# Hybrid encoder block: contraction groups of 2, 4, 4, 4, 2 row blocks, silu(c) from a replicated row, x turned in parts

## The chip, the core and the metric

The kernel runs on one core of a Trainium2 chip. The metric is the time of one execution on the device, in microseconds (us); less is better. Engines are named as in the profile: PE multiplies matrices, DVE and ACT work on vectors, SP issues the DMAs.

## What is computed

One encoder layer on 256 tokens of 2048 channels, in float32:

```python
mod = silu(c) @ w_ada + b_ada                       # 6 parts of 2048
sh1, sc1, gt1, sh2, sc2, gt2 = split(mod, 6)
h = rmsnorm(x, g_pre_mix) * (1 + sc1) + sh1
proj = h @ w_in                                     # 10752 columns
# HGRN2 on q, f_fwd, f_bwd, i, g (1024 columns each) -> y_a
# windowed attention on q, k, v                      -> y_b
y = (sigmoid(gate_a) * y_a + sigmoid(gate_b) * y_b) @ w_out
x = x + gt1 * rmsnorm(y, g_post_mix)
h = rmsnorm(x, g_pre_ffn) * (1 + sc2) + sh2
y = expert_choice_ffn(h)                            # 16 experts, 32 tokens each
x = x + gt2 * rmsnorm(y, g_post_ffn)
```

## The kernel before

**Weights** come as 1 MB tiles (128 partitions, 2048 floats each), each into one of 25 slots, through one DMA queue that SP issues. The list `prog` is the order of use and of loading. "A" tiles are blocks of `w_ada` for shift and scale of the first norm, "B" tiles are blocks of the other four parts, "W" tiles hold 4 row blocks (of 128 rows) of 512 columns of `w_in`.

**Modulation.** `ada` (L399) multiplies an A or B tile with silu(c) and sums along the row, on DVE. silu(c) stands on all partitions (`CR`): `expand` (L293) makes it from a column array by four products on PE that ACT copies out (L298). It does so at the start and once more in the last expert, where the last four B tiles are used.

**Start.** `norm_x` squares both halves of x on ACT (L323), scales all of x (L330, ACT), transposes it on PE (L334) and copies it out (L336, ACT), giving `nT`. `rotary` makes the angle tables (DVE lines around L382, two sines on ACT). `mod_gain` (L404, L406) finishes shift and scale, and `make_h` applies them for the row blocks of one group (L416 on ACT) and splits the result into an upper and a lower part (L417 on ACT, L418 on DVE).

**First stage.** The contraction has 16 row blocks, taken in groups by `GRP`. In each group ten chunks of 512 columns (`EARLY`: f0, b0, f1, b1, q0, q1, hg0, hg1, v0, v1) are multiplied. A weight tile is split by `split`, per 1024 floats: ACT casts the upper part (L433), DVE subtracts the lower (L434), into one of four ring slots. `prod` makes three passes on PE (L181) into one of two PSUM pairs that alternate. The sum is then evicted to a slab (L766, ACT); in later groups it is first reloaded from the slab (L763, ACT); in the last group the eviction applies sigmoid or silu (L768), except for v0 and v1. The A tiles of the next group's row blocks are spread over the chunks of a group; before the first group stand the 8 A tiles of its own. The last group carries 8 B tiles instead.

**After it** come HGRN2 (`hgrn`, from L503, with scans on DVE at L507) beside the other chunks of `w_in`, attention, the branches, the router and the 16 experts.

Programs are scheduled: the order of each engine's instructions is fixed before the run, and is in parts not that of the source. Every engine works through its own list in order.

Of the kernel before, what the change touches and what calls it, by code (L numbers as in the profile page):

```python
# [22 lines left out]
D = 2048  # L23
T = 256
NT = 2
# [14 lines left out]
GRP = [4, 4, 4, 4]  # L40
# [6 lines left out]
# column constants: one [128, W] array  # L47
# [8 lines left out]
# w_in chunks of 512 columns: (kind, first column); "t" comes out as channels x tokens  # L56
# [14 lines left out]
CHUNKS = EARLY + LATE  # L71


class Mem:
    """SBUF in slots of 8 KB per partition; every tenant of a slot is its own tile, and a
    tenant's first write is issued after the one of the tenant before it. A tile gets the
    slot that has been free for longest, so that its load can run ahead."""
# [30 lines left out]
class Ring:  # L108
    """slots that serve one kind of tile in turn"""
# [18 lines left out]
def block_kernel(ctx: ExitStack, tc: tile.TileContext, x, cols, pos, ident_in, hmask, bmask, smask, w_ada, w_in, w_a, w_b, w_out, w_r, w_gu, w_dn, out):  # L128
# [9 lines left out]
    # ---------------- PSUM: two pairs of banks, a ring of three banks, one more bank  # L138
# [16 lines left out]
    # ---------------- stream of weight tiles, 1 MB each, in the order of use  # L155
# [27 lines left out]
    # ---------------- constants  # L183
# [6 lines left out]

    ident = cp.tile([128, 128], F32, name="ident")
# [20 lines left out]
    def table(name="natural_log_exp_and_others"):  # L212
        """the table of ScalarE for what follows on it"""
        S.preload_act_table_set(name)

    def rsqrt(ss, n):
        """sums of D squares -> 1 / rms: exponential of the logarithm, one Newton step"""
        l, r, t, v = tiny(n), tiny(n), tiny(n), tiny(n)
        S.activation(l, ss, AF.Ln, scale=1.0 / D, bias=epsc)
        S.activation(r, l, AF.Exp, scale=-0.5)  # L220
        V.tensor_scalar(v, ss, 1.0 / D, EPS, ALU.mult, ALU.add)
        V.tensor_tensor(t, r, r, ALU.mult)
        V.scalar_tensor_tensor(t, t, -0.5, v, ALU.mult, ALU.mult)
# [6 lines left out]
    prog = [("X",)]  # L230
# [6 lines left out]
    for g in range(NG):  # L237
# [6 lines left out]
        nt, ne = len(todo), len(EARLY)  # L244
        for i, n in enumerate(EARLY):
            prog.append(("W", n, G0[g], GRP[g]))
            k = min(nt, (i + 1) * nt // (ne - NA0)) - min(nt, i * nt // (ne - NA0))
            prog += todo[:k]
            todo = todo[k:]
        prog += todo  # L250
    def mix(items, n, m):
        """items with the next n of the ada tiles spread over the first m"""
# [16 lines left out]
    def src(it):  # L269
        k = it[0]  # L270
        if k in "AB":
            return w_ada[it[1], it[2]]
        if k == "W":
            return w_in[CHUNKS.index(it[1]), it[2] // 4]
        return {"YA": w_a, "YB": w_b, "O": w_out}[k][it[1], it[2]]

    stream += [src(it) for it in prog if it[0] not in "HX"]
# [7 lines left out]
    def spread(c4, w, b=None):  # L285
        """four columns -> their 512 values along the free axis, on all partitions, in a bank"""
# [6 lines left out]
    def expand(c16, name):  # L293
        """a [128, 16] column array -> the 2048 values along the free axis, on all partitions"""
# [7 lines left out]
    # ---------------- x -> n = x / rms(x), transposed  # L302
# [7 lines left out]
    # silu(c) on every partition  # L310
    sig = tiny(16)
    S.activation(sig, col("c"), AF.Sigmoid)
    V.tensor_tensor(sig, sig, col("c"), ALU.mult)
    CR = expand(sig, "crow")
# [3 lines left out]
    def norm_x():  # L318
        for tt in range(NT):
            nc.sync.dma_start(X[tt], x[tt])  # L320
        scr = mem.get([D], F32, "sq")
        for tt in range(NT):
            S.activation(scr, X[tt], AF.Square, accum_out=ssq[:, tt:tt + 1])  # L323
        mem.put(scr)
        rs = rsqrt(ssq, NT)
        for k2 in range(8):
            if k2 % 2 == 0:
                for tt in range(NT):
                    xp = X[tt][:, 256 * k2:256 * k2 + 512]
                    S.activation(xp, xp, AF.Copy, scale=rs[:, tt:tt + 1])  # L330
# [5 lines left out]
            S.copy(NTl[k2 // 4][:, 2 * (k2 % 4):2 * (k2 % 4) + 2, :].rearrange("p a b -> p (a b)"), b)  # L336
        mem.put(*X)
# [9 lines left out]
    # lower bounds of the forget gates: softmax over the two depths  # L347
# [19 lines left out]
    # rotary tables: cos, sin per token  # L367
# [25 lines left out]
    # ---------------- modulation columns  # L393
# [3 lines left out]
    def ada(p, k, t):  # L397
        """block k of 128 channels of modulation part p"""
# [40 lines left out]
    def prod(ps, parts, kind, lhh, lhl, k0, first, last):  # L439
        """ps += (row blocks from k0 of the activations)^T (weight tile)"""  # L440
# [24 lines left out]
    # ---------------- slabs: outputs of the input projection  # L465
# [18 lines left out]
    # ---------------- HGRN2: two heads (half hf) of chunk i  # L484
    def hgrn(i, hf):
# [47 lines left out]
        for j in range(2):  # L533
# [6 lines left out]
            # scores of both directions, transposed: within the chunks, and from one chunk of a pair to the other  # L540
# [17 lines left out]
            # keys scaled to the end of the pair, queries to its start  # L558
# [23 lines left out]
        # per-head norm over the channels (partitions), gate  # L582
# [40 lines left out]
    def heads_t(x3, h, o):  # L623
        """channels x tokens of heads h, h+1 of a token-major slab"""
# [69 lines left out]
    # ---------------- the run through the weight tiles before the experts  # L694
# [146 lines left out]
    for it in prog:  # L841
# [7 lines left out]
        if it[0] == "X":  # L849
            norm_x()  # L850
# [11 lines left out]
        else:  # L862
            pend.append((it, split(t)))
# [9 lines left out]
    # ---------------- residual, second norm  # L873
# [31 lines left out]
    # ---------------- router  # L905
# [41 lines left out]
    def gather(e):  # L947
        """the 32 rows of expert e: channels x rows, normed, with gain and shift"""
# [23 lines left out]
    def combine_weights(e):  # L972
        # combine weights [4 copies of 32 slots, tokens]
# [18 lines left out]
    # ---------------- experts  # L992
    for e in range(NE):
        if e == NE - 1:
            JK = RT[:, 192:704].rearrange("p (t c) -> p t c", t=2)
            sf8 = tiny(16).rearrange("p (t c) -> p t c", t=2)
            CR = expand(sig, "crow")
# [34 lines left out]
        for cb in range(8):  # L1032
# [4 lines left out]
            # 256 columns: sums over a quarter of the rows each in the four groups of 32 partitions,  # L1037
            # which the combine adds up
# [27 lines left out]
    # ---------------- second residual  # L1066
# [37 lines left out]
def finish_deps(tc, nc, mem, mark, pairs):  # L1104
    """the order of a slot's tenants; a table's load stays between its neighbours on ScalarE"""
# [28 lines left out]
def layout(inputs):  # L1134
# [23 lines left out]
    def chunks(w, starts):  # L1158
# [4 lines left out]
    win = chunks(f("w_in").reshape(D, -1), [CH[n][1] for n in CHUNKS])  # L1163
# [16 lines left out]
        "x": f("x").reshape(NT, P, D), "cols": cols, "pos": posn, "ident": np.eye(P, dtype=np.float32),  # L1180
        "hmask": hm, "bmask": bmk, "smask": smk, "w_ada": ada, "w_in": win, "w_a": w_a,
# [21 lines left out]
```

## Time and profile before

| what | us |
|---|---|
| median of 3 runs | 1747.77 |
| lowest, highest | 1747.76, 1747.88 |
| the profiled execution, from first to last instruction | 1746.1 |
| outside this span (median less span) | 1.67 |
| PE busy | 1442.9 |
| DVE busy | 782.3 |
| ACT busy | 555.9 |

The profiled execution's own time is 1747.8 when the 1.67 us outside its span are added, so its span stands for the median. The page's slices show three parts: up to some 830 us PE is busy in nearly every slice, and DMA in 60 to 100% of them; from there to the end DMA is busy without a gap at 419 GB/s while PE waits part of the time. In the first slice of 44 us the engines wait for each other.

### The profile page before, as it was taken

How to read it: one execution, taken by the hardware profiler on the slowest of the kernel's cores; microseconds unless marked ns; L12 is line 12 of the kernel's file. 1: busy time of each engine (PE TensorE's matmuls, PEld its weight loads, DVE VectorE, ACT ScalarE, POOL GpSimd, SP SyncE). 2: the span in 40 equal slices, each digit the busy share in tenths (PEclk: the TensorE clock that was granted, in tenths of full speed). 3: DMA queues.
4: the chain of work that ended last, by engine and by line, in shares of the span. 5: the costliest groups of instructions: out<-in, count | busy, mean ns of one | idle time of the engine just before them, and what ended most of it. 6: DMA issues, size and time to landing. Idle time of an engine off the chain costs nothing.

```text
span 1746.1 us, 24226 instructions
## 1 busy us (share of the span) xinstructions
PE 1442.9 (83%) x10230; PEld 924.5 (53%) x10230; DVE 782.3 (45%) x1048; ACT 555.9 (32%) x865; POOL 0.2 (0%) x4
## 2 busy tenths in 40 slices
PE   4999999999999999997877777776867777677674
PEld 2989997789999998862322312221322232122212
DVE  7777788999977897443111101111111111011115
ACT  6467776655564444441200100000000001000012
POOL 0000000000000000000000000000000000000000
PEclk8999999999999999998998879888897879788987
DMA  9978966766978788776999999999999999999996
GB/s 388 419 293 321 345 255 234 271 245 272 351 271 356 309 352 323 303 306 269 419 419 419 420 419 419 420 420 419 419 419 420 419 419 419 419 419 419 419 419 254
DMA packets 88796, 633.98 MB, mean 363 GB/s; under 512 B 9968, under 2 KB 10480, under 8 KB 11888
## 3 DMA queue, kind: packets, MB, share of 16 engines
q1 hardware_dynamic: 88688, 632.44, 89.7%
q8 instruction: 80, 1.31, 0.3%
q14 instruction: 28, 0.23, 0.0%
HBM read 630.30 MB, written 2.10 MB: 362 GB/s over the span
## 4 chain that ended last, share of the span: by engine, by line
PE 44%; DMA 43%; DVE 8%; ACT 3%; issue 2%; SPq 0%; DVEq 0%; ACTq 0%
PE PS L181 43%; DMA w<-in_w_gu_dram 32%; DMA w<-in_w_dn_dram 9%; DVE w L399 2%; DVE hl L434 1%; DMA w<-in_w_ada_dram 1%; ACT ew L1048 1%; ACT hl L433 1%; DVE F L507 0%; DMA w<-in_w_in_dram 0%; PE PS L1020 0%; ACT ew L1017 0%; DVE x L1086 0%; PE PS L681 0%; PE PS L892 0%
## 5 line engine op out<-in xcount | busy, mean ns | idle before, releaser
L181 PE MATMUL PS<-w,rt 128*32 128x512 f32 x2048 | 325.4, 711 | 141.4 <-DMA w<-in_w_gu_dram 140.1
L181 PE MATMUL PS<-hh,hl 128*128 128x256 f32 x2048 | 383.1, 287 | 13.2 <-ACT hl L433 8.9
L181 PE MATMUL PS<-hl,hl 128*128 128x256 f32 (+1 forms) x1184 | 356.7, 301 | 0.0
L434 DVE TENSOR_TENSOR hl<-w,hl 128x1024 fp32r<-128x1024 f32 x232 | 281.1, 1223 | 118.9 <-ACT hl L433 118.7
L181 PEld LDWEIGHTS PS<-hh,hl 128*128 128x128 f32 x2048 | 324.8, 194 | 15.5 <-ACT hl L433 9.3
L433 ACT CAST hl<-w 128x1024 fp32r<-128x1024 f32 x232 | 241.1, 1048 | 164.8 <-PE PS L181 156.5
L181 PEld LDWEIGHTS PS<-w,rt 128*32 128x32 f32 x2048 | 55.7, 116 | 368.2 <-DMA w<-in_w_gu_dram 301.3
L181 PEld LDWEIGHTS PS<-hl,hl 128*128 128x128 f32 x1184 | 228.7, 193 | 7.2 <-issue 0.7
L399 DVE SCALAR_TENSOR_TENSOR w<-w,crow 128x2048 f32<-128x2048 f32 x96 | 218.8, 2285 | 7.6 <-DMA w<-in_w_ada_dram 4.8
L181 PE MATMUL PS<-ew,rt 128*128 128x256 f32 x512 | 157.7, 434 | 70.0 <-ACT ew L1048 70.0
L1059 DVE TENSOR_TENSOR acc<-acc,PS 128x512 f32<-128x512 f32 x120 | 82.5, 688 | 261.4 <-PE PS L181 261.4
L181 PEld LDWEIGHTS PS<-ew,rt 128*128 128x128 f32 x512 | 94.2, 204 | 146.6 <-ACT ew L1048 137.9
L181 PE MATMUL PS<-w,ew 128*32 128x256 f32 x2048 | 151.5, 415 | 13.9 <-DVE ew L1026 13.9
L1048 ACT COPY ew<-PS 128x256 f32<-128x256 f32 x128 | 47.5, 371 | 259.5 <-PE PS L181 259.5
L1026 DVE TENSOR_TENSOR ew<-ew,PS 128x256 f32<-128x256 f32 x16 | 6.7, 421 | 235.2 <-ACT ew L1025 235.2
L181 PE MATMUL PS<-hl,hh 128*128 128x512 f32 x320 | 103.8, 401 | 5.3 <-DVE hl L434 2.9
L952 DVE TENSOR_SCALAR rt<-ct,rt,small 128x32 f32<-128x32 f32 x32 | 9.4, 300 | 208.4 <-PE PS L181 208.3
L181 PEld LDWEIGHTS PS<-w,ew 128*32 128x32 f32 x2048 | 56.7, 115 | 85.8 <-issue 47.5
L958 ACT COPY ew<-PS 128x512 f32<-128x512 f32 x15 | 8.8, 586 | 268.2 <-PE PS L181 268.2
L1017 ACT COPY ew<-PS 128x512 f32<-128x512 f32 x16 | 9.4, 586 | 232.5 <-PE PS L181 232.5
L181 PE MATMUL PS<-hl,mh 128*128 128x512 f32 x256 | 81.1, 396 | 0.8 <-ACT hl L433 0.7
L181 PEld LDWEIGHTS PS<-hl,hh 128*128 128x128 f32 x320 | 60.1, 191 | 19.9 <-DVE hl L434 4.9
(243 smaller groups left out, 1191.0 us busy)
## 6 DMA issues: line engine op xcount, KB each, us to landing
w<-in_w_gu_dram SPq DMA_DIRECT2D x256, 1024.0 KB, 19.9
w<-in_w_dn_dram SPq DMA_DIRECT2D x128, 1024.0 KB, 19.9
w<-in_w_ada_dram SPq DMA_DIRECT2D x96, 1024.0 KB, 7.0
w<-in_w_in_dram SPq DMA_DIRECT2D x84, 1024.0 KB, 7.4
w<-in_w_out_dram SPq DMA_DIRECT2D x16, 1024.0 KB, 10.6
w<-in_w_a_dram SPq DMA_DIRECT2D x8, 1024.0 KB, 6.5
w<-in_w_b_dram SPq DMA_DIRECT2D x8, 1024.0 KB, 8.3
x<-in_x_dram SPq DMA_DIRECT2D x4, 1024.0 KB, 8.1
```

Source lines behind the costliest of these rows:

```text
L181: E.matmul(o, l, r, start=start, stop=stop, skip_group_check=True, **kw)
L399: V.scalar_tensor_tensor(t, t, 1.0, CR, ALU.mult, ALU.mult, accum_out=MOD[:, p, k:k + 1])
L433: S.copy(hl[:, 0, :], w)
L434: V.tensor_tensor(hl[:, 1, :], w, hl[:, 0, :].bitcast(F32), ALU.subtract)
L952: V.tensor_scalar(oh[:, tt, :], io, pm3[:, tt, e:e + 1], r2[:, tt:tt + 1], ALU.is_equal, ALU.mult)
L958: S.copy(g, b)
L1017: S.copy(gu, b)
L1026: V.tensor_tensor(he, sl_, b3[:, :, 64:128], ALU.mult)
L1048: S.copy(y, b[:, :256])
L1059: V.tensor_tensor(a, a, p3, ALU.add)
```

## The change

- `GRP` is 2, 4, 4, 4, 2 in place of 4, 4, 4, 4: five groups, the first and the last of two row blocks.
- In the groups of two a weight tile holds two row blocks of two chunks ("P" items, `w_e2`, built on the host): one load and one `split` feed the products of a pair of chunks. The groups of four use `w_e4`, tiles as before.
- 4 A tiles stand ahead of the first group. The 8 of the second group are spread over its five P items. The groups of four carry 8, 8 and 4, the last group 8 B tiles.
- `CR` is a 1 MB array that holds c on every row. It is loaded by one DMA ahead of x and given silu in place by ACT, at the start and again in the last expert.
- The first half of x is squared on ACT, the second on DVE. `turn_x` takes 512 columns at a time: the first part before the first group, the others after the second, third and fourth P item's A tiles by the source. For these DVE scales x and copies one of two banks out.
- `rotary` stands after the first chunk of the second group by the source.

```diff
-GRP = [4, 4, 4, 4]
+GRP = [2, 4, 4, 4, 2]
+PAIRS = [EARLY[i:i + 2] for i in range(0, len(EARLY), 2)]
...
+    CR = mem.get([D], F32, "crow")
+    nc.sync.dma_start(CR, crow)
...
-        for i, n in enumerate(EARLY):
-            prog.append(("W", n, G0[g], GRP[g]))
+        items = [("P", i, G0[g]) for i in range(len(PAIRS))] if GRP[g] == 2 else [("W", n, G0[g], GRP[g]) for n in EARLY]
+        nt, ne = len(todo), len(items)
+        for i, it in enumerate(items):
+            prog.append(it)
...
+            if g == 0 and 0 < i < 4:
+                prog.append(("X", i))
+            if g == 1 and i == 0:
+                prog.append(("R",))
...
-    sig = tiny(16)
-    S.activation(sig, col("c"), AF.Sigmoid)
-    V.tensor_tensor(sig, sig, col("c"), ALU.mult)
-    CR = expand(sig, "crow")
+    S.activation(CR, CR, AF.Silu)
...
+        S.activation(scr, X[0], AF.Square, accum_out=ssq[:, 0:1])
+        V.scalar_tensor_tensor(scr, X[1], 1.0, X[1], ALU.mult, ALU.mult, accum_out=ssq[:, 1:2])
+        mem.put(scr)
+        return rsqrt(ssq, NT)
+
+    def turn_x(c):
+
         for tt in range(NT):
...
+            xp = X[tt][:, 512 * c:512 * c + 512]
+            if c:
+                V.tensor_scalar(xp, xp, rs[:, tt:tt + 1], None, ALU.mult)
+            else:
+                S.activation(xp, xp, AF.Copy, scale=rs[:, tt:tt + 1])
+        for k2 in (2 * c, 2 * c + 1):
...
+            if c and k2 % 2:
+                V.tensor_copy(o, b)
+            else:
+                S.copy(o, b)
...
-            pend.append((it, split(t)))
+            parts = split(t)
+            if it[0] == "P":
+                pend += [(("W", n, it[2], 2), [part]) for n, part in zip(PAIRS[it[1]], parts)]
+            else:
+                pend.append((it, parts))
...
-            CR = expand(sig, "crow")
+            CR = mem.get([D], F32, "crow")
+            nc.sync.dma_start(CR, crow)
+            S.activation(CR, CR, AF.Silu)
```

Three places show how instructions move. First DVE ahead of the first group's products, before:

```order
L399 SCALAR_TENSOR_TENSOR w_215,MOD<-w_215,crow_88 128x2048
L399 SCALAR_TENSOR_TENSOR w_218,MOD<-w_218,crow_88 128x2048
L404 TENSOR_TENSOR MOD<-MOD,ct 128x4
L399 SCALAR_TENSOR_TENSOR w_221,MOD<-w_221,crow_88 128x2048
L404 TENSOR_TENSOR MOD<-MOD,ct 128x4
```

The same place after the change, from the first A tile on (w_132 to w_141 are the four A tiles, x_89 and x_90 the halves of x):

```order
L420 SCALAR_TENSOR_TENSOR w_132,MOD<-w_132,crow_67 128x2048
L343 TENSOR_SCALAR x_89<-x_89,small 128x512
L343 TENSOR_SCALAR x_90<-x_90,small 128x512
L343 TENSOR_SCALAR x_89<-x_89,small 128x512
L420 SCALAR_TENSOR_TENSOR w_135,MOD<-w_135,crow_67 128x2048
L354 COPY nT_82<-PS 128x512
L343 TENSOR_SCALAR x_90<-x_90,small 128x512
L420 SCALAR_TENSOR_TENSOR w_138,MOD<-w_138,crow_67 128x2048
L354 COPY nT_83<-PS 128x512
L425 TENSOR_TENSOR MOD<-MOD,ct 128x2
L420 SCALAR_TENSOR_TENSOR w_141,MOD<-w_141,crow_67 128x2048
```

Eight A tiles in a row have become four, with scalings of x and copies out of PSUM between them; two more scalings and the third copy follow before the subtractions.

Second, ACT inside the first group, before (hl are the upper parts of weight tiles, F and Q slabs):

```order
L433 CAST hl_370<-w_368 128x1024
L433 CAST hl_373<-w_368 128x1024
L766 COPY F_55_376<-PS 128x1024
L433 CAST hl_431<-w_429 128x1024
L433 CAST hl_434<-w_429 128x1024
L766 COPY F_55_376<-PS 128x1024
```

After (w_193 is the second P tile, w_270 the third):

```order
L787 COPY F_24_161<-PS 128x1024 x2
L454 CAST hl_195<-w_193 128x1024
L454 CAST hl_198<-w_193 128x1024
L787 COPY F_33_226<-PS 128x1024 x2
L454 CAST hl_272<-w_270 128x1024
L454 CAST hl_275<-w_270 128x1024
```

Before, the two casts of the next chunk stand ahead of the eviction of the chunk that PE works on. After, both evictions of a pair stand ahead of the first cast of the next pair.

Third, ACT in the last group, before:

```order
L768 ACTIVATE F_42_255<-PS 128x1024
L433 CAST hl_2082<-w_2077 128x1024
L763 COPY PS<-F_55_376 128x1024
L433 CAST hl_2140<-w_2138 128x1024
L768 ACTIVATE F_55_376<-PS 128x1024
```

After:

```order
L789 ACT_TABLE_LOAD
L789 ACTIVATE F_24_161<-PS 128x1024
L454 CAST hl_2323<-w_2321 128x1024
L789 ACTIVATE F_24_161<-PS 128x1024
L784 COPY PS<-F_33_226 128x1024
L454 CAST hl_2326<-w_2321 128x1024
L784 COPY PS<-F_33_226 128x1024
L524 ACTIVATE T_268_2513<-F_24_161,OM,NOM 128x256 x2
L789 ACTIVATE F_33_226<-PS 128x1024
```

Per chunk ACT has an eviction, a reload and two casts before, and an eviction, a reload and one cast after; the chunk's products are half as many, and the reload of F_33 stands behind the second eviction of F_24.

## Rows read from the trace of the kernel before

**Rows 1.** Busy time of each engine by stage: start, first group, the other groups, HGRN2, experts. Columns: stretch, its length, PE, PEld, DVE, ACT, POOL busy (instructions), granted PE clock, DMA share, GB/s.

```profile
0.00:39.10 39.10, 15.30 (x40) 7.46 (x40) 26.72 (x57) 23.34 (x40) 0.20 (x4) 0.86 0.95 385
39.10:103.50 64.40, 60.14 (x433) 57.61 (x433) 48.22 (x49) 37.85 (x47) 0.00 (x0) 0.95 0.96 390
103.50:276.10 172.60, 172.60 (x1297) 166.92 (x1298) 129.34 (x129) 127.31 (x143) 0.00 (x0) 0.99 0.79 303
276.10:513.90 237.80, 231.33 (x1583) 207.58 (x1583) 221.69 (x323) 144.76 (x230) 0.00 (x0) 0.99 0.71 269
830.00:1735.00 905.00, 661.74 (x4804) 229.57 (x4802) 142.68 (x240) 93.94 (x245) 0.00 (x0) 0.86 1.00 415
```

**Rows 2.** The chain of work that ended last, its pieces up to the first scan of HGRN2: start, length, engine, what.

```profile
17.08 2.30 DVE w L399 x2
20.26 13.27 DVE w L399 x12
33.72 2.22 DVE w L399 x2
36.42 1.09 ACT nT L416 x2
39.11 1.22 PE PS L181 x4
...
100.53 1.99 ACT hl L433 x2
103.49 167.18 PE PS L181 x1272
270.69 1.02 ACT Q L766
271.72 1.28 ACT L214
275.73 1.22 DVE F L507
```

**Rows 3.** Groups of instructions by line and shape: busy, mean ns of one, then the idle time of the engine before them and what ended it.

```profile
L399 DVE SCALAR_TENSOR_TENSOR w<-w,crow 128x2048 f32<-128x2048 f32 x96 | 218.8, 2285 | 7.6 <-DMA w<-in_w_ada_dram 4.8 <-ACT crow L298 2.8
L434 DVE TENSOR_TENSOR hl<-w,hl 128x1024 fp32r<-128x1024 f32 x232 | 281.1, 1223 | 118.9 <-ACT hl L433 118.7
L896 DVE COPY yg<-PS 128x512 f32<-128x512 f32 x4 | 2.8, 690 | 2.4 <-PE PS L892 2.4
L382 DVE SCALAR_TENSOR_TENSOR rot<-rot 128x128 f32<-128x128 f32 x6 | 1.7, 291 | 0.2
L1086 DVE SCALAR_TENSOR_TENSOR x<-acc,small,x 128x512 f32<-128x512 f32 x8 | 5.5, 746 | 0.0
L416 ACT ACTIVATE nT<-nT,MOD 128x256 f32<-128x256 f32 x16 | 8.8, 595 | 5.8 <-DVE MOD L406 5.8
L763 ACT COPY PS<-F 128x1024 f32<-128x1024 f32 x12 | 12.1, 1018 | 0.0
L768 ACT ACT_TABLE_LOAD x2 | 2.6, 1283 | 0.0
```

**Rows 4.** Instructions on DVE in order of time, a cast of a mask: start, length, instruction.

```profile
264.77 0.42 DVE L344 CAST bm<-mtmp 128x512 uint8<-128x512 f32 x1
```

**Rows 5.** Instructions on ACT in order of time: the square of the first half of x at the start, a chunk inside the first group, and the passage from the first group to the second. In brackets the idle time before and what ended it.

```profile
7.38 1.91 ACT L323 ACTIVATE sq<-x 128x2048 f32<-128x2048 f32 x1 [4.13 <-DMA x<-in_x_dram]
82.65 1.01 ACT L766 COPY HG<-PS 128x1024 f32<-128x1024 f32 x1 [2.85 <-PE PS L181]
83.56 2.00 ACT L433 CAST hl<-w 128x1024 fp32r<-128x1024 f32 x2
88.41 1.02 ACT L766 COPY HG<-PS 128x1024 f32<-128x1024 f32 x1 [2.85 <-PE PS L181]
99.32 1.01 ACT L766 COPY Q<-PS 128x1024 f32<-128x1024 f32 x1
102.42 1.96 ACT L763 COPY PS<-F 128x1024 f32<-128x1024 f32 x2
```

**Rows 6.** Instructions on ACT in order of time, the end of the last group: v0's eviction is the copy at 270.69.

```profile
253.70 1.03 ACT L768 ACTIVATE Q<-PS 128x1024 f32<-128x1024 f32 x1 [0.83 <-PE PS L181]
254.62 1.04 ACT L433 CAST hl<-w 128x1024 fp32r<-128x1024 f32 x1
255.56 1.02 ACT L763 COPY PS<-HG 128x1024 f32<-128x1024 f32 x1
270.69 1.02 ACT L766 COPY Q<-PS 128x1024 f32<-128x1024 f32 x1 [1.61 <-PE PS L181]
273.02 0.60 ACT L503 ACTIVATE T<-F,OM,NOM 128x256 f32<-128x256 f32 x1
```

**Rows 7.** Busy time of the engines in single microseconds, columns as in rows 1: six us after the first product, and the passage from the first group to the second.

```profile
44.00:45.00 1.00, 1.00 (x6) 1.00 (x6) 1.00 (x2) 0.00 (x0) 0.00 (x0) 0.50 1.03 426
45.00:46.00 1.00, 1.00 (x10) 1.00 (x9) 1.00 (x1) 0.96 (x1) 0.00 (x0) 0.87 0.96 401
104.00:105.00 1.00, 1.00 (x7) 1.00 (x6) 1.00 (x1) 0.39 (x1) 0.00 (x0) 0.50 0.17 33
107.00:108.00 1.00, 1.00 (x11) 1.00 (x10) 1.00 (x1) 0.00 (x0) 0.00 (x0) 1.00 0.99 401
```

More of the change, by code (lines that the diff above doesn't have):

```diff
@@ L127, in block_kernel @@
 @with_exitstack
-def block_kernel(ctx: ExitStack, tc: tile.TileContext, x, cols, pos, ident_in, hmask, bmask, smask, w_ada, w_in, w_a, w_b, w_out, w_r, w_gu, w_dn, out):
+def block_kernel(ctx: ExitStack, tc: tile.TileContext, x, cols, crow, pos, ident_in, hmask, bmask, smask, w_ada, w_e2, w_e4, w_in, w_a, w_b, w_out, w_r, w_gu, w_dn, out):
     nc = tc.nc
@@ L229, in block_kernel @@
     G0 = [sum(GRP[:g]) for g in range(NG)]
-    prog = [("X",)]
+    prog = [("X", 0)]
     a_tiles = [("A", p, k) for k in range(KT) for p in range(2)]
@@ L243, in block_kernel @@
             b_tiles = b_tiles[BE:]
-        nt, ne = len(todo), len(EARLY)
-        for i, n in enumerate(EARLY):
-            prog.append(("W", n, G0[g], GRP[g]))
+        items = [("P", i, G0[g]) for i in range(len(PAIRS))] if GRP[g] == 2 else [("W", n, G0[g], GRP[g]) for n in EARLY]
+        nt, ne = len(todo), len(items)
+        for i, it in enumerate(items):
+            prog.append(it)
             k = min(nt, (i + 1) * nt // (ne - NA0)) - min(nt, i * nt // (ne - NA0))
@@ L272, in src @@
             return w_ada[it[1], it[2]]
+        if k == "P":
+            return w_e2[min(it[2], 1), it[1]]
+        if k == "W" and it[1] in EARLY:
+            return w_e4[EARLY.index(it[1]), it[2] // 4]
         if k == "W":
-            return w_in[CHUNKS.index(it[1]), it[2] // 4]
+            return w_in[LATE.index(it[1]), it[2] // 4]
         return {"YA": w_a, "YB": w_b, "O": w_out}[k][it[1], it[2]]
-    stream += [src(it) for it in prog if it[0] not in "HX"]
+    stream += [src(it) for it in prog if it[0] not in "HXR"]
     tail = prog_tail
@@ L321, in norm_x @@
         scr = mem.get([D], F32, "sq")
-        for tt in range(NT):
[L323 to L330, printed above, removed]
+        S.activation(scr, X[0], AF.Square, accum_out=ssq[:, 0:1])
[3 more added lines that the diff above has]
+    def turn_x(c):
+        for tt in range(NT):
+            xp = X[tt][:, 512 * c:512 * c + 512]
[4 more added lines that the diff above has]
+        for k2 in (2 * c, 2 * c + 1):
             b = bank()
@@ L335, in norm_x @@
                                 X[tt][:, 128 * (2 * k2 + j):128 * (2 * k2 + j) + 128], ident)
-            S.copy(NTl[k2 // 4][:, 2 * (k2 % 4):2 * (k2 % 4) + 2, :].rearrange("p a b -> p (a b)"), b)
-        mem.put(*X)
+            o = NTl[k2 // 4][:, 2 * (k2 % 4):2 * (k2 % 4) + 2, :].rearrange("p a b -> p (a b)")
+            if c and k2 % 2:
+                V.tensor_copy(o, b)
+            else:
+                S.copy(o, b)
+        if c == 3:
+            mem.put(*X)
     def load_masks():
@@ L849, in block_kernel @@
         if it[0] == "X":
-            norm_x()
+            if it[1] == 0:
+                rs = norm_x()
+            turn_x(it[1])
+            continue
+        if it[0] == "R":
             rotary()
@@ L1161, in chunks @@
         return np.stack([w4[..., s:s + 512].transpose(0, 2, 1, 3).reshape(k, P, 2048) for s in starts])
-    win = chunks(f("w_in").reshape(D, -1), [CH[n][1] for n in CHUNKS])
+    wi = f("w_in").reshape(D, -1)
+    wl = chunks(wi, [CH[n][1] for n in LATE])
+    we = wi.reshape(KT, P, -1)
+    we = np.stack([we[:, :, CH[n][1]:CH[n][1] + 512] for n in EARLY], axis=2)
+    we4 = we[2:14].reshape(3, 4, P, len(EARLY), 512).transpose(3, 0, 2, 1, 4).reshape(len(EARLY), 3, P, 2048)
+    we2 = np.stack([we[0:2], we[14:16]]).reshape(2, 2, P, len(PAIRS), 2, 512)
+    we2 = we2.transpose(0, 3, 2, 4, 1, 5).reshape(2, len(PAIRS), P, 2048)
     four = [0, 512, 1024, 1536]
@@ L1179, in layout @@
     return {
-        "x": f("x").reshape(NT, P, D), "cols": cols, "pos": posn, "ident": np.eye(P, dtype=np.float32),
-        "hmask": hm, "bmask": bmk, "smask": smk, "w_ada": ada, "w_in": win, "w_a": w_a,
+        "x": f("x").reshape(NT, P, D), "cols": cols, "crow": np.broadcast_to(f("c").reshape(1, D), (P, D)), "pos": posn, "ident": np.eye(P, dtype=np.float32),
+        "hmask": hm, "bmask": bmk, "smask": smk, "w_ada": ada, "w_e2": we2, "w_e4": we4, "w_in": wl, "w_a": w_a,
         "w_b": w_b, "w_out": w_o, "w_r": w_r, "w_gu": gu, "w_dn": dn,
```

## The prediction

> **What bounds the kernel now.** I read the busy times by stage first, then the chain of work that ended last, then ACT and DVE instruction by instruction where the chain changes engine. The stages have different limits [rows 1]. Up to 39.1 us nothing is multiplied but transposes; PE is busy 15.3 of 39.1 us. In the first group PE is busy 60.1 of 64.4 us, in the three others 172.6 of 172.6. HGRN2 then keeps DVE busy for 221.7 of 237.8 us, and in the experts DMA is the limit (share 1.00 at 415 GB/s). So a shift of the front passes through: HGRN2 begins later or earlier as a whole, and so do the stages behind it. That the experts would absorb a shift of some us nothing shows: their loads wait for slots that are freed in the order of the work.
>
> The chain [rows 2] goes at the start through DVE: eight products with silu(c) from 17.08 to 35.9 us, then the gain, two ACT instructions, and the first product at 39.11. It stays on PE until 270.69, when v0 is evicted, but for one break: v1 of the first group is evicted at 99.32 [rows 5], two casts and a reload follow, and PE goes on at 103.49, 4.2 us later. Everywhere else ACT waits for PE, 2.85 us per chunk [rows 5]: PE sets the pace, 5.76 us a chunk (88.41 less 82.65). This is the margin that the change spends.
>
> **The start: PE begins earlier.** Removed: the four spread products and copies that hold the first product of DVE until 17.08 [rows 2], and four of eight products at 2.21 us each (13.27 us for six [rows 2], mean 2.285 of which the engine overlaps a little [rows 3]). Added ahead of x is a load of 1 MB, 2.5 us at the 415 GB/s of rows 1. x was squared at 7.38 [rows 5], so its first half comes at about 9.2 behind the row, its second at 11.7, the first A tile at 14.2. ACT has silu(c) at 8.7, loads a table (1.28 [rows 3]) and squares the first half until 12.3. DVE squares the second behind it (one scratch tile) until 14.65, and the root is done at 15.7. Then DVE has, in its order, four products (8.84), six scalings, three copies from PSUM (0.69 each as L896 [rows 3], 2.07) and the gains (0.3). The scaling of 128x512 is not in the trace with this operation. From below it is the cast of L344 at 0.42 [rows 4], from above the two-source L1086 at 0.75 [rows 3]; I take 0.42, since both read one source, so 2.5 us, or 4.5 at the upper end. That ends at 29.1. Identity (0.6 [rows 3]), cast and the remaining steps give a first product at 30.65, **8.4 us earlier** (6.4 with 0.75).
>
> Beside those rows, the Trainium skill ("VectorE: DVE Perf Modes", "The perf-mode tier table") gives float32 `tensor_scalar` between SBUF tiles twice the rate of `tensor_tensor`, which speaks for 0.42; by a single rate it would be 30.65 + 2.0. No scaling of this shape stands in the trace yet.
>
> **The first group gives it back.** Two row blocks for ten chunks are 28.8 us at PE's pace (172.6 us [rows 1] for twelve). Before, the casts of the next chunk stand ahead of the eviction in ACT's order. After, both evictions of a pair stand ahead of the next pair's first cast, as the second piece of the order shows. PE's last product of a pair is followed by an eviction (0.92 from 83.56 less 82.65 [rows 5]), a cast (1.0) and the semaphores: PE stands still 2.0 us. The lower part then needs a subtraction of 1.22 [rows 3], of which two matmuls hide a little: up to 2.9. I take 2.4 for three of the four borders, 7.2. At the fourth border the rotary table (1.28 [rows 3]), sine and two Identities of 0.6 stand between eviction and cast: 4.0 us. At the end of the group the eviction of v0 waits on ACT behind four casts and two Identities; with the reload that leaves 2.7 us, where before there were 4.2. DVE has two products and two subtractions per pair, 2 x 2.21 + 2 x 1.18 = 6.8 us, and 12 rotary steps of up to 0.29 [rows 3] once; with PE at 5.76 + 2.4 it does not come to bind.
>
> The clock: after the wait ahead of 39.11 it was at 0.50, which is the lower level of 1.2 GHz, until 45 [rows 7], and after the 4.2 us gap again at 104, back at 1.00 by 107. The first costs 3.0 us here as it did before, the 4.0 us gap another 1.5. So the second group starts at 30.65 + 28.8 + 3.0 + 7.2 + 4.0 + 2.7 + 1.5 = 77.85. Before, with the same two row blocks still uncounted, that point is 103.49 - 28.8 = 74.7. **+3.2 us**; all 8.4 are lost and a little more. The bounds are 2.0 and 2.9 per border (1.5 either way), the scalings (+2.0), and a clock that drops at every border or at none (+4.5, -1.5).
>
> **The groups of four** keep the pace of 57.5 us per group [rows 1]: DVE has 20 subtractions and 8 products, 41.3 us of that. Only the reload of f0 stands later against v0's eviction in ACT's order, **+1.2 us** at two borders.
>
> **The last group: ACT becomes the bound.** A chunk is 2.88 us of PE now. ACT has a cast, a reload and an activation per chunk, about 0.95 each back to back (255.56 less 254.62 is 0.94 [rows 6]), 2.85 us; before there was one cast more but 5.76 us of PE, so ACT waited for PE. On top come two table loads, 2.6 us [rows 3], and three Identity-like steps of HGRN2 at 0.6 [rows 6], which before lay in ACT's waits. That alone is 28.5 + 2.6 + 1.7 = 32.8 us against 28.8. Two reloads behind the second eviction of a slab (third piece of the order) stop PE for 2 to 2.8 us each, partly the same time: I take 34.0, **+5.2 us**; the bounds are 28.8 + 1.0 and 36.
>
> Of ACT's table loads the trace shows 1.28 at 271.72 and the next instruction at 273.02 [rows 2, 6], 1.30 in all. Beside this the Trainium skill ("ScalarE: Activation LUTs", "What ACT_TABLE_LOAD costs") states a load of 1283 ns and as much again for a drain, 2.66 us a switch; by it three loads on the path would add 4.1, for 1764.5. The trace disagrees on the drain, so the sum keeps 1.30.
>
> **HGRN2** waits for v0. Before, one chunk of four row blocks remained at its eviction; now one of two: PE's work ahead of it is **2.75 us** more. One B product that stood behind the first scan's start comes ahead of it, and DVE is the bound there: **-2.2 us**.
>
> **The last expert** loads the row again, 1 MB more at the full share of DMA: **+2.5 us** [rows 1]; it is between 0, if it slips into a gap of the tail, and 2.5. The expansion that it replaces lay beside transfers and gains nothing.
>
> **Sum.** 3.2 + 1.2 + 5.2 + 2.75 - 2.2 + 2.5 = +12.65. The profiled execution's span is 1746.1 and 1.67 lie outside it, 1747.8 together, the median. The forecast is 1747.8 + 12.65 = **1760.5** (rounded). Its own bounds: front -3 to +6.5, last group -4.2 to +2, row -2.5 to 0, give 1751 to 1769.
>
> **Rivals.** *Faster: the early start passes on.* If the casts ran ahead at the borders (the first P tiles are loaded in time, four ring slots hold two pairs) and the last group kept PE's pace, the front would be 30.65 + 28.8 + 3.0 + 4.2 = 66.7, -8.0, and the sum -8.0 - 2.2 + 2.5 = -7.7: 1740. For it speaks that PE never waits in 172.6 us of such products [rows 1]; against it the order on ACT, which no faster engine changes. It decides when the gap per border is under 0.5 us. *No change: half of it.* Borders of 1.0 us in place of 2.4 (-4.2), no clock drop (-1.5) and a last group at 31 (-3) give 1751.8, the row hidden 1749.3: about 1750. *Slower still: the clock.* If each border sends PE back to 1.2 GHz as the gap of 4.2 us did [rows 7], with 1.5 us each, three more drops in the first group and two in the last give +7.5: 1768. A gap of 2 us is not in these rows, so it stays open. *The change doesn't do what it says:* if DVE reached its first product as late as 17.08 (a late row), the start would move 1.4 us, 1762, inside the forecast's bounds.
>
> **How the numbers follow.** Forecast 0.58, faster 0.14, no change 0.13, clock 0.15. A measurement can tell 0.2%, 3.5 us, from no change: "same" is 1744.3 to 1751.3. The forecast's lower edge touches it and gives nothing to it. So faster 0.14, same 0.13, slower 0.73. The range drops the rival of 1740, and little at the upper end: 1747 to 1770.
>
> **What would show it.** First product on PE near 30.7: the start is right. Waits of PE of 2 to 3 us between pairs, released by the casts, and the second group near 78: the first group is right. If it starts near 67, the faster rival is. ACT busy without a wait in the last group, and v0's eviction 10 to 14 us later than 270.69: the last group is right. The last expert's tiles later by 2.5 us than the ones before it: the row. What would make it wrong most easily is the length of the gaps between pairs, which rests on an order and on no row of this kernel.

## The result and the profile after

| | before | after |
|---|---|---|
| median, us | 1747.76 | 1767.92 |
| lowest, highest, us | 1747.03, 1747.88 | 1765.24, 1772.54 |
| span of the profiled execution, us | 1746.1 | 1766.1 |

The ratio is 1.0117, 95% interval 1.0103 to 1.0131: the change costs some 20 us, where 12.7 were forecast. The profiled execution after took 1767.93 us, its span and 1.8 us outside.

The first stages of the changed kernel, busy time as in [rows 1] (start, first group, groups of four):

```profile
0.00:31.00 31.00, 7.99 (x34) 5.90 (x34) 19.41 (x41) 14.45 (x20) 0.20 (x4) 0.88 0.94 380
31.00:81.00 50.00, 39.15 (x214) 35.10 (x214) 36.91 (x50) 26.30 (x36) 0.00 (x0) 0.80 0.91 358
81.00:254.80 173.80, 171.78 (x1298) 165.42 (x1299) 130.10 (x128) 124.69 (x141) 0.00 (x0) 1.00 0.84 309
```

The start is 8 us shorter. The first group now takes 50 us for half the work that took 64.4, at a granted clock of 0.80, with PE busy 39 of 50 us. The three groups of four are nearly what they were (173.8 against 172.6).

The chain of work that ended last, up to the first scan, which answers to [rows 2]:

```profile
31.04 7.06 PE PS L182 x46
38.12 1.01 ACT F L787
39.13 1.91 ACT hl L454 x2
41.08 6.92 PE PS L182 x44
...
81.05 46.35 PE PS L182 x384
...
197.51 57.26 PE PS L182 x432
254.80 1.01 ACT Q L787
...
257.69 1.28 ACT L789
258.99 1.03 ACT F L789
...
291.83 1.22 DVE F L528
```

Before, the chain went through PE from 103.49 to 270.69 in one piece. Now it goes through an eviction and two casts at each border of the first group, and through ACT in the last group. ACT there, which answers to [rows 6] (idle time ahead in brackets):

```profile
257.69 1.28 ACT L789 ACT_TABLE_LOAD   x1
258.99 1.03 ACT L789 ACTIVATE F<-PS 128x1024 f32<-128x1024 f32 x1
259.91 1.04 ACT L454 CAST hl<-w 128x1024 fp32r<-128x1024 f32 x1
...
261.87 1.02 ACT L784 COPY PS<-F 128x1024 f32<-128x1024 f32 x1
...
265.16 1.09 ACT L524 ACTIVATE T<-F,OM,NOM 128x256 f32<-128x256 f32 x2 [0.38 <-DVE hl L455]
...
280.80 1.03 ACT L789 ACTIVATE HG<-PS 128x1024 f32<-128x1024 f32 x1 [1.39 <-PE PS L182]
...
286.78 1.02 ACT L787 COPY Q<-PS 128x1024 f32<-128x1024 f32 x1 [0.28 <-PE PS L182]
```

Before, ACT waited for PE in every chunk here; now its pauses from 257.69 to the eviction of v0 at 286.78 are 0.38, 1.39 and 0.28 us, 2.05 in all, and PE stands still twice for a reload by ACT:

```profile
262.94 0.39 PE L182 MATMUL PS<-hh,hl 128*128 128x256 f32 x1 [2.09 <-ACT PS L784]
277.57 0.38 PE L182 MATMUL PS<-hh,hl 128*128 128x256 f32 x1 [2.50 <-ACT PS L784]
```

A few instants, read from the timelines and the tables of each line, show where the 20 us arise. Each row's difference less that of the row above is what the stretch between them costs. The first product is the start of the steady stream; after the change two products ran already at 29.93, and PE then waited 0.31 us.

| instant | before | after | difference |
|---|---|---|---|
| first product | 39.11 | 31.04 | -8.1 |
| second group begins (before: same row blocks left, 103.49 - 28.8) | 74.7 | 81.05 | +6.35 |
| v0 evicted | 270.69 | 286.78 | +16.1 |
| first transposition for the second norm | 775.8 | 792.9 | +17.1 |
| gather for the last expert | 1623.7 | 1642.9 | +19.2 |
| second residual begins | 1732.6 | 1752.6 | +20.0 |

### The profile page after: what moved, and what is told of

It is laid out like the page before. It is cut to its first block, busy times and chain, and to the rows that moved or that the text cites. A ratio compares the mean times of both kernels' runs of the same rounds, so it can differ in the third digit from the quotient of the medians.

```text
span 1766.1 us, 24202 instructions
## 1 busy us (share of the span) xinstructions
PE 1439.8 (82%) x10214; PEld 919.5 (52%) x10214; DVE 782.9 (44%) x1053; ACT 567.0 (32%) x867; POOL 0.2 (0%) x4
## 4 chain that ended last, share of the span: by engine, by line
PE 44%; DMA 39%; DVE 8%; ACT 6%; issue 2%; SPq 0%; ACTq 0%; DVEq 0%
PE PS L182 42%; DMA w<-in_w_gu_dram 32%; DMA w<-in_w_dn_dram 6%; DVE w L420 2%; ACT hl L454 2%; DVE hl L455 1%; ACT ew L1079 1%; DMA w<-in_w_ada_dram 1%; ACT PS L784 1%; DMA x<-in_x_dram 1%; DVE F L528 0%; PE PS L1051 0%; ACT ew L1048 0%; ACT rt L1093 0%; DVE acc L1090 0%
## 5 line engine op out<-in xcount | busy, mean ns | idle before, releaser
L182 PE MATMUL PS<-w,rt 128*32 128x512 f32 x2048 | 338.7, 735 | 149.4 <-DMA w<-in_w_gu_dram 148.2
L182 PE MATMUL PS<-hh,hl 128*128 128x256 f32 x2048 | 387.4, 289 | 13.7 <-ACT hl L454 6.8
L182 PE MATMUL PS<-ew,rt 128*128 128x256 f32 x512 | 151.8, 421 | 70.5 <-ACT ew L1079 70.4
L182 PE MATMUL PS<-w,ew 128*32 128x256 f32 x2048 | 146.0, 403 | 13.9 <-DVE ew L1057 13.9
L182 PE MATMUL PS<-hl,hh 128*128 128x512 f32 x320 | 107.7, 414 | 10.5 <-ACT hl L454 6.0
```

Source lines behind the costliest of these rows:

```text
L182: E.matmul(o, l, r, start=start, stop=stop, skip_group_check=True, **kw)
```

## The experiments

All changes are to the changed kernel, but for the one to the kernel before (x9_row). Each was timed in several rounds beside runs of the kernel before.

**x1_order: casts ahead of evictions in the first group.**

```diff
+            lastcast[0] = latest(mybir.EngineType.Activation)      # in split, behind the cast
...
                     S.copy(s, ps)
+                    if first:
+                        pairs.append((latest(mybir.EngineType.Activation), lastcast[0]))
```

> In the first group the second chunk of a pair is evicted after the casts of the next pair. Theory (ACT's order stops PE at each border, and each stop lets the clock fall): the stops of 2.05 us before 40.1, 50.0 and 60.1 us are gone, the granted clock stays at 1.00 from 37 us up to the rotary tables, the second group begins at 69 to 73 us instead of 81.05, and the time falls by 8 to 11 us to about 1758. Rival (the stops are those of late weight tiles or of DVE's subtractions behind the products with silu(c)): the second group begins at 78 us or later and the time stays within 2 us of 1768.

Measured: median 1765.48 us, 1.0089 of before [1.0075, 1.0102]; the second group begins at 78.88. The stop at the first border is gone and the one at the second is 0.68 us, but at the third it is 4 us. PE's products behind its waits, in order of time (in brackets the idle time and its releaser):

```profile
45.78 0.50 PE L182 MATMUL PS<-hh,hl 128*128 128x256 f32 x2 [0.68 <-DVE hl L458]
55.80 0.80 PE L182 MATMUL PS<-hh,hl 128*128 128x256 f32 x2 [4.01 <-DVE hl L458]
66.67 0.50 PE L182 MATMUL PS<-hl,hh 128*128 128x512 f32 x1 [2.78 <-ACT hl L456]
78.88 0.58 PE L182 MATMUL PS<-hh,hl 128*128 128x256 f32 x1 [4.52 <-ACT PS L787]
```

The releaser of the 4 us is DVE: two products with silu(c) and twelve rotary steps are queued ahead of the fourth pair's subtraction. So ACT's order was the first limit, and DVE stood right behind it. Neither text holds alone: the stops went with the order, as the theory has it, but the queue that the rival names took most of the gain, and the second group begins where the rival had it. The first scan came only 0.3 us earlier than in the changed kernel (291.53), the first transposition 6.7 us (786.2; from the one to the other it is 494.7 us against 501.1), and the second residual 1.8 us (1750.7): in its last expert the clock was at the lower level, see below.

**x2_fill: products of the identity in the stops.**

```diff
+    def fill():
+        for _ in range(6):
+            mm(obank[:, 0:128], ident, ident, True, True)
...
+                if first and n in ("f1", "q0", "hg0", "v0"):
+                    after(mybir.EngineType.PE, fill)
+                    after(mybir.EngineType.PE, lambda: prod(ps, parts, kind, lh, ll, k0, first, True))
```

> Six products of the identity with itself stand on PE at each border between pairs of the first group, where PE waits for ACT; all else is as in the changed kernel. Theory (a stop of 2 us costs a second time because the clock falls after it): the clock stays at 1.00 at the borders, a pair takes 8.0 to 8.3 us instead of 9.9, the second group begins at 74 to 77 us instead of 81.05, the time falls by 4 to 6 us to about 1763. Rival (PE is slow behind a stop because it waits for the subtractions of the lower parts): a pair stays at 9.9 us and the time at 1768.

Measured: 1767.6 us, 1.0107 [1.0089, 1.0124]: no gain in time, and a pair takes 8.54 us, a little above the theory's 8.0 to 8.3; but the mechanism shows. The clock (last columns: granted clock, DMA share, GB/s) behind the first border, in the changed kernel:

```profile
42.00:44.00 2.00, 2.00 (x11) 2.00 (x11) 2.00 (x2) 0.00 (x0) 0.00 (x0) 0.50 1.00 414
```

and with the stop filled:

```profile
42.00:44.00 2.00, 2.00 (x19) 2.00 (x18) 2.00 (x2) 0.00 (x0) 0.00 (x0) 1.00 0.98 406
```

19 products in place of 11 in the same 2 us. PE's products behind its waits show the period of a pair; shortly behind each border there is a second wait of 0.21 us. Filled:

```profile
41.17 0.39 PE L182 MATMUL PS<-hh,hl 128*128 128x256 f32 x1 [0.21 <-ACT hl L454]
...
49.71 0.39 PE L182 MATMUL PS<-hh,hl 128*128 128x256 f32 x1 [0.21 <-ACT hl L454]
```

and in the changed kernel:

```profile
40.13 0.38 PE L182 MATMUL PS<-hh,hl 128*128 128x256 f32 x1 [2.05 <-ACT hl L454]
41.08 0.58 PE L182 MATMUL PS<-hh,hl 128*128 128x256 f32 x1 [0.21 <-ACT hl L454]
...
50.98 0.57 PE L182 MATMUL PS<-hh,hl 128*128 128x256 f32 x1 [0.21 <-ACT hl L454]
...
71.89 0.80 PE L182 MATMUL PS<-hl,hh 128*128 128x512 f32 x1 [3.85 <-ACT hl L454]
...
81.05 0.38 PE L182 MATMUL PS<-hh,hl 128*128 128x256 f32 x1 [0.20 <-ACT PS L784]
```

8.54 us (49.71 less 41.17) against 9.90 (50.98 less 41.08): a stop of 2.05 us costs another 1.4 by the clock. The gain did not reach the second group (80.36 against 81.05), because the edit moved both reloads behind both casts at the end of the group: there PE waited 4.2 us.

**x3_expand: no second load of the row.**

```diff
-            CR = mem.get([D], F32, "crow")
-            nc.sync.dma_start(CR, crow)
-            S.activation(CR, CR, AF.Silu)
+            sig = tiny(16)
+            S.activation(sig, col("c"), AF.Silu)
+            CR = expand(sig, "crow")
```

> The last expert makes silu(c) on all partitions by the spread products of before, without the second load of the row. Theory (that load costs its transfer, because DMA sets the pace there): the time falls by 2.5 to 3 us to about 1765, and the distance between the gathers of the first and of the last expert is that of before, 809.7 us, rather than 811.4. Rival (the load lies beside other work): no change, 1768.

Measured: 1762.94 us, 1.0084 [1.007, 1.0097]: 5 us less than the changed kernel, more than expected, and the distance of the gathers did not change (811.4). Only part of it is the row. From the first transposition to the second residual it is 958.0 us (789.1 to 1747.1), in the changed kernel 959.7: 1.7. The rest lies in HGRN2, in a part of the source that the two kernels share, where the profiled execution of the changed kernel had the lower clock for a time:

```profile
330.00:340.00 10.00, 10.00 (x43) 8.21 (x42) 10.00 (x12) 6.95 (x7) 0.00 (x0) 0.83 0.81 304
```

and this one not:

```profile
330.00:340.00 10.00, 10.00 (x49) 8.38 (x48) 10.00 (x12) 6.86 (x7) 0.00 (x0) 1.00 0.78 301
```

From the first to the last scan it is 113.9 us there and 110.1 here, 113.0 before. By the rows the fall of the clock there is not the whole of these 3.8 us: from the second pair of scans to the third (325.89 to 361.31 there, 325.77 to 359.58 here) the difference is 1.6 us. The other 2 come between the third pair and the fourth, where both executions have a granted clock of 0.83 from 370 to 380 us; their cause stays open.

**x4b_merge6: the last two groups as one of six row blocks.** GRP is 2, 4, 4, 6, the last group takes W, P, W tiles for a pair of chunks, and the ring has 6 slots.

```diff
+        elif GRP[g] == 6:
+            for i, (a, b) in enumerate(PAIRS):
+                items += [("W", a, G0[g], 6), ("P", i, G0[g] + 4), ("W", b, G0[g], 6)]
...
-NHL = 4
+NHL = 6
```

> Groups of 2, 4, 4, 6: the last two groups are one, six weight halves in the ring in place of four. Theory (in a group of two ACT sets the pace, and v0 is evicted late): the last group runs at PE's pace of 8.64 us a chunk with ACT waiting, v0 is evicted at 275 to 278 us instead of 286.78, and the time falls by 9 to 12 us to about 1757. Rival (HGRN2 starts earlier but PE's other chunks set the end of that stage, so that only PE's stops in the last group are won): v0 as early, time down by 5 us at most, 1763.

Measured: 1785.36 us, 1.0216 [1.0202, 1.023], far off both. In the last group PE did keep its pace, as the theory has it (two evictions 8.64 us apart, with waits for PE ahead of them):

```profile
224.24 1.02 ACT L796 ACTIVATE F<-PS 128x1024 f32<-128x1024 f32 x1 [1.83 <-PE PS L182]
...
232.88 1.02 ACT L796 ACTIVATE F<-PS 128x1024 f32<-128x1024 f32 x1 [1.82 <-PE PS L182]
```

but it began late: at the end of the first group PE stood still for 6.71 us, so that the second group began at 84.20, and on the passage into the last group, with twelve A products and six row blocks of h ahead, for 4.11 us. v1 of the group ahead was evicted at 206.96, in the changed kernel at 197.39. v0 followed at 284.56, only 2.2 us earlier than there. The larger loss came behind it: 4.9 us more from the first scan to the last, and from the last scan to the first transposition 399.9 us in place of 387.2. The ring's two slots more leave two fewer for loads; that this is the cause of the 12.7 us was not tried.

**x5_rot: x1_order, and rotary held behind the first chunk of the second group.**

```diff
-            rotary()
+            after(mybir.EngineType.DVE, rotary)
```

> As x1_order, and the rotary steps begin on DVE only where the source has them, behind the first chunk of the second group. Theory (once ACT's order no longer stops PE, DVE does, and its rotary steps and ACT's sine table stand in the way of the gain for the second group): the second group begins at 70 to 73 us, where x1_order had 78.88 and the changed kernel 81.05, and the time is 1756 to 1760. Rival (DVE's eight products with silu(c) and ten subtractions fill the group by themselves): the second group begins at 76 us or later and the time is 1763 or more.

Measured: 1756.45 us, 1.0051 [1.0038, 1.0064], 9 less than x1_order; the second group begins at 71.97, and both are in the range of the theory. Of the 9 us, 5.6 are there at the first transposition (780.66); the rest lies behind it, where x1_order had the lower clock in its last expert. The waits of PE in the first group:

```profile
44.77 0.50 PE L182 MATMUL PS<-hh,hl 128*128 128x256 f32 x2 [0.69 <-DVE hl L458]
51.47 0.51 PE L182 MATMUL PS<-hh,hl 128*128 128x256 f32 x2 [0.69 <-DVE hl L458]
59.68 0.50 PE L182 MATMUL PS<-hl,hh 128*128 128x512 f32 x1 [2.67 <-ACT hl L456]
71.97 0.58 PE L182 MATMUL PS<-hh,hl 128*128 128x256 f32 x1 [4.62 <-ACT PS L787]
```

The 4 us at DVE are gone. What stays is the wait for shift and scale ahead of the last pair and the end of the group.

**x6_last: only the last group.** As x1_order for the last group, every second reload on DVE, four of its eight B products in the group ahead.

```diff
-                    S.copy(ps, s)
+                    if last and EARLY.index(n) % 2:
+                        V.tensor_copy(ps, s)
+                    else:
+                        S.copy(ps, s)
```

> Only the last group differs from the changed kernel: casts ahead of evictions in ACT's order, every second reload on DVE, and four of the eight B products in the fourth group. Theory (ACT sets the pace of the last group): v0 is evicted at 280 to 283 us instead of 286.78, the waits of PE in that group fall below 2 us, and the time falls by 3 to 6 us to about 1763. Rival (PE's stops there come from the order of reloads alone, or the stage behind takes the time back): v0 before 284 but the end of the input projection and the time as before, 1767 or more.

Measured: 1767.63 us, 1.0111 [1.0097, 1.0124], v0 evicted at 287.17: no gain, and v0 later than both texts have it. PE still stands still twice in that group. The first stop, 2.35 us, waits for a reload that is left on ACT, behind a table load and two evictions; the second, 1.69 us, for one that now stands in DVE's queue behind products:

```profile
270.40 2.29 DVE L424 SCALAR_TENSOR_TENSOR w<-w,crow 128x2048 f32<-128x2048 f32 x1
...
273.75 1.22 DVE L792 COPY PS<-Q 128x1024 f32<-128x1024 f32 x1
```

**x7_all: x5_rot, x6_last, x3_expand, and the first chunk's reload ahead of the second's casts.**

```diff
-            while len(pend) > LA:
+            while len(pend) > (0 if it[0] == "W" and it[1] == "f0" else LA):
```

> x5_rot, x6_last and x3_expand together, and the reload of the first chunk of a group ahead of the casts of the second. If the three losses (first group, last group, row in the last expert) are all there is, the second group begins at 68 to 71 us, v0 is evicted at 268 to 274 us, and the time is 1744 to 1752, on both sides of the kernel before. If something else of groups of two costs time (loads that come in another order, HGRN2 that starts later), it stays above 1755.

Measured: 1745.67 us, 0.9987 of before [0.9978, 0.9996]. The second group begins at 70.54, v0 is evicted at 271.43, both in the range, and the first transposition is at 772.2, in the kernel before at 775.8. PE's stops at the reloads of the last group are down to 0.63 and 0.65 us.

**x8_g4: groups of 4, 4, 4, 4, all else as in the changed kernel.**

```diff
-GRP = [2, 4, 4, 4, 2]
+GRP = [4, 4, 4, 4]
```

> Groups of 4, 4, 4, 4 as before, all else as in the changed kernel: the row for silu(c), x turned in parts, rotary late, the row again in the last expert. Theory (the start is set by the products of silu(c) on DVE, eight of them again; the row itself wins 1.4 us and the scalings and copies on DVE cost 4 to 5): the first product is at 39 to 42 us, and the time is 1749 to 1754, most of it the row in the last expert. Rival (the row and the parts are what made the start earlier): the first product at 31 to 36 us and a time below 1746.

Measured: 1755.24 us, 1.004 [1.0027, 1.0052], a little above the theory's range. The first product is at 40.96, 1.85 us later than before: the row and the turning in parts together win nothing without the smaller first group, the scalings and copies stand between the products on DVE:

```profile
17.86 1.27 DVE L343 TENSOR_SCALAR x<-x,small 128x512 f32<-128x512 f32 x3
19.05 2.28 DVE L420 SCALAR_TENSOR_TENSOR w<-w,crow 128x2048 f32<-128x2048 f32 x1
...
21.26 0.68 DVE L354 COPY nT<-PS 128x512 f32<-128x512 f32 x1
```

The first transposition is 1.4 us later than before, the second residual 7.2: the larger part of this kernel's loss is in the last expert.

**x9_row: the kernel before, with the row in the last expert.** The edit is that of x3_expand, the other way round.

> The kernel before with one change: in the last expert silu(c) comes as a loaded row with ACT's silu, in place of the spread products. Theory (the row lengthens a stage that DMA bounds): the landing of the last gate and up tile and the end move by 2.5 to 3 us, the time is 1750 to 1751.5; more only if PE's clock in the last expert falls for it, up to 1755. Rival (the row costs nothing, the changed kernel's loss there is of the clock alone): 1747.5 to 1748.5.

Measured: 1753.93 us, 1.003 [1.0019, 1.004]; single executions from 1748.55 to 1755.41. The median is above the theory's 1750 to 1751.5, in the part up to 1755 that it keeps for a fall of PE's clock. The profiled execution is the fastest: from the first transposition to the second residual 959.9 us, in the kernel before 956.8. So in this execution the row costs 3.1 us, near its transfer, as the theory has it. The median is 5.8 us above that of the kernel before (1748.16); whether the other 2.7 are such a fall no trace shows, as no slower execution was profiled.

**x10_nolast: x7_all without its changes in the last group.**

> x7_all without its changes in the last group (reloads on DVE, B products moved forward, casts ahead of evictions there). Theory (the last group costs 5 us because ACT sets its pace): v0 is evicted 5 to 7 us later than the 271.43 us of x7_all, and the time is 1750 to 1753. Rival (the gain of x7_all is that of the first group and of the row alone): 1745 to 1747.

Measured: 1752.24 us, 1.002 [1.0011, 1.0029]: 6.6 us more than x7_all, with v0 at 278.28, 6.85 later. The theory's range holds: the last group is a loss of its own. Its three changes were taken out together, so what each of them is worth is not shown.

**x11_fill: x7_all with products of the identity in the two stops that are left in front.** The fill is that of x2_fill with 8 products, ahead of the fifth pair and of the second group.

> x7_all with eight products of the identity in each of the two stops of PE that are left in front (2.7 us each, before the fifth pair and before the second group). All else keeps its order. Theory (a stop costs a second time by the clock, 1.4 us each): the clock stays at 1.00 behind both, the second group runs on 2 to 3 us earlier, the time is 1742 to 1744. Rival (the work behind waits for DVE and ACT anyway): 1745 to 1746.

Measured: 1743.69 us, 0.9974 of before [0.9964, 0.9984], 2.0 less than x7_all, with v0 at 269.01, 2.4 earlier: the theory holds. The clock from 72 to 74 us, behind the start of the second group, is 1.00 in place of 0.50. The clock behind the fifth border, in x7_all:

```profile
62.00:64.00 2.00, 2.00 (x6) 1.61 (x5) 1.62 (x4) 1.49 (x3) 0.00 (x0) 0.50 1.07 442
```

and filled:

```profile
62.00:64.00 2.00, 2.00 (x9) 1.65 (x10) 1.73 (x3) 2.00 (x4) 0.00 (x0) 1.00 0.98 406
```

## Why the prediction was right, and where it was too small

The direction was right, and so was the mechanism in front and in the last group; 1767.9 us lie inside the range of 1747 to 1770, 7.5 above the forecast of 1760.5. HGRN2 came out with the other sign. Term by term, measured from the instants above:

| term | forecast | measured |
|---|---|---|
| first product | -8.4 | -8.1 |
| start and first group together | +3.2 | +6.35 |
| borders between groups of four | +1.2 | +1.4 |
| last group and v0's later eviction | +7.95 | +8.35 |
| HGRN2 to the second norm | -2.2 | +1.0 |
| from there to the end | +2.5 | +2.9 |

**The start.** First product forecast at 30.65, measured at 31.04. (The forecast's own steps from 15.7 on add up to 0.3 more than it has; it left out the gains.) Of the two prices for a scaling of 128x512, 0.42 was right: three stand in 1.27 us. The Trainium skill ("VectorE: DVE Perf Modes", "The perf-mode tier table") has float32 `tensor_scalar` between SBUF tiles at twice the rate of `tensor_tensor`; the trace agrees as far as it goes, with 0.40 from one to the next against 0.66 for the residual's instructions that read two sources (six of them in 4.06 us, from 1752.56 on). x8_g4 shows that the 8.1 us come from four products fewer, and that the row with the turning in parts is worth nothing there.

**The first group** is a term that was sized too small. The step that took 2.4 us per border had the stop right (2.05, and a short second one of 0.21; the fourth was forecast at 4.0 and measured at 3.85) and put a fall of the clock only behind the fourth. It falls behind each of them: 1.4 us more per border (x2_fill), 4.2 at three. With the clock held, the fifth pair's first product came at 68.94, without at 71.89. That the term is short by only 3.15 is in part luck, since two other steps were too large. The slow stretch behind the first product was put at 3.0; 46 products took 7.06 us, where at PE's pace (24 in 2.88) they take 5.5, so 1.5. The end of the group was put at a stop of 2.7 and 1.5 for the clock; the last pair took 9.16 us (81.05 less 71.89) in place of 5.76, so 3.4 in all, and its stop was 0.20. The statement that DVE "does not come to bind" held only because ACT held PE: x1_order, with ACT out of the way, waited 4 us for DVE, and x5_rot freed them. So the rotary steps on DVE, which the sum had at zero, cost nothing that shows as long as ACT held PE, and stood in the way once ACT's order was mended. The bounds of the front have a slip too: the upper one is 6.5, while its three parts (1.5, 2.0 and 4.5) add up to 8.0.

**The last group** behaved as forecast: ACT's pauses up to v0's eviction were 2.05 us in 29, PE's two stops for its reloads 2.09 and 2.50 (forecast 2 to 2.8 each), and x10_nolast against x7_all prices it at 6.6 us. x6_last shows that moving every second reload to DVE is not enough: one stop stayed at ACT, the other moved to DVE's queue. A table load took 1.30 us to the next instruction's start here too (257.69 to 258.99). By the drain that the Trainium skill adds to it ("ScalarE: Activation LUTs", "What ACT_TABLE_LOAD costs") it would be 2.66; no run shows that.

**HGRN2.** The gain of 2.2 us is not in the profiled execution: from first scan to first transposition it is 501.1 us, before 500.1. In five other kernels whose source for the last group is that of the changed kernel (x1_order, x2_fill, x3_expand, x5_rot, x10_nolast) the stretch is 494.7 to 497.2 us, and in x9_row, whose source is that of the kernel before up to the last expert, 498.1. So a gain of the forecast's size is likely, and something hides it in the profiled execution. Part of that is the fall of the clock at 330 to 340 us: in x3_expand PE stopped at the same place, 2.02 us long against 2.22, and the clock stayed at 1.00. It explains 1.6 us; the rest stays open.

**The row.** The stretch behind the second norm grew by 2.9, where 2.5 was forecast, but not all of it is the row: without the row (x3_expand) 1.7 of it goes and 1.2 stays, and the row alone (x9_row) costs 3.1. Its transfer at 415 GB/s, 2.5 us, lies between.

The rival "Slower still: the clock" gave 1768 and the measured time is 1767.9. That the numbers agree is luck, for it was half right: three more falls in the first group, but none in the last, where the clock stayed at 1.00; its other 3 us are those of HGRN2. The rival by which the early start passes on needed gaps under 0.5 us; they were 2.05.

## What to carry to other kernels

Halving the work between two evictions halves the time in which the evicting engine must also prepare what comes next: count that engine's instructions per piece against the multiplier's time per piece, in the order in which they are queued, before making pieces smaller. A stop of the multiplier is to be priced with the slower stretch that can follow it, and filling it can win that part back. When one engine's order is mended, look at once at the next engine's queue: here both had to be put right (x1_order, x5_rot) before the earlier start reached the end.

## What the runs showed of the hardware

- In the changed kernel each stop of PE of 2.05 us between stretches of steady products was followed by a stretch at a granted clock of 0.50 (all of 42 to 44 us), the lower level of 1.2 GHz; filled with products of the identity, the clock stayed at 1.00 and 1.4 us per stop were won (x2_fill; x11_fill won 2.4 by v0's eviction with two stops of 2.7 filled). The length of a stop alone does not decide it. In the last group PE stood still for 2.50 us, from 275.07 to 277.57, and the clock stayed up:

```profile
274.00:276.00 2.00, 1.07 (x9) 0.86 (x8) 0.29 (x1) 2.00 (x3) 0.00 (x0) 1.00 0.90 348
276.00:278.00 2.00, 0.43 (x3) 0.43 (x4) 0.94 (x1) 2.00 (x3) 0.00 (x0) 1.00 0.99 414
278.00:280.00 2.00, 2.00 (x19) 2.00 (x18) 1.23 (x1) 1.40 (x2) 0.00 (x0) 1.00 0.64 270
```

  And in x4b_merge6, whose first group has the same stops, the clock was at 0.50 from 44 to 46 us behind the first (the next border 10.01 us on) and stayed at 1.00 behind the second (the next border 8.52 us on). What decides it is not shown.

```profile
51.38 0.38 PE L182 MATMUL PS<-hh,hl 128*128 128x256 f32 x1 [2.05 <-ACT hl L461]
...
59.90 0.38 PE L182 MATMUL PS<-hh,hl 128*128 128x256 f32 x1 [2.05 <-ACT hl L461]
```

```profile
53.00:55.00 2.00, 2.00 (x19) 2.00 (x18) 2.00 (x2) 0.00 (x0) 0.00 (x0) 1.00 0.27 33
```

- In the last expert the clock is at either level when the last gate and up tile lands. In x1_order it was at 0.50, and eight products took 1.98 us; in x9_row it was at 1.00, and they took 1.11:

```profile
1711.62 1.98 PE PS L182 x8
```

```profile
1699.06 1.11 PE PS L181 x8
```

  From these products to the second residual it is 39.1 us in x1_order and 34.3 in x9_row (34.3 also before and after). The difference, 4.8 us, is of the size of that between single executions of one kernel (x9_row, 1748.55 to 1755.41); whether it is the cause there, and what decides the level, stays open.
